# A hybrid decoder layer on one core: the second halo sum from raw weight rows, four steps moved in attention, and the y splits set ahead of the turns

## The chip, the cores and the metric

The kernel runs on one NeuronCore of a Trainium2 chip. The core has TensorE (matrix products, PE in the profile, with its weight loads as PEld), VectorE (DVE), ScalarE (ACT), GpSimd (POOL), and SyncE (SP), whose queue issues nearly all of this kernel's DMAs. The metric is the device time of one execution in microseconds (us), lower is better. The time shown is the median of three runs.

## The reference

One layer over 16 meta tokens and 1024 real tokens of width 1024, in float32. The parts around the change are these:

```python
h = jnp.concatenate([meta, x], axis=1)
for l in range(DEPTH):
    xn = rms_norm(h, mix_pre_g[l])
    proj = xn @ w_in[l]
    ...
    y_ssd = ssd_mixer(z, xbc, dt_raw, ssd_conv_w[l], ssd_conv_b[l], ssd_dt_bias[l],
                      ssd_a_log[l], ssd_d[l], ssd_norm_g[l])
    y_sb = rms_norm(stick_breaking_attention(q, k, v).reshape(Bsz, L, SB_WIDTH), sb_norm_g[l])
    mix = jnp.concatenate([y_ssd, y_sb], axis=-1) @ w_out[l]
    h = h + rms_norm(mix, mix_post_g[l])
    xn = rms_norm(h, ffn_pre_g[l])
    gu = xn @ w_up[l]
    g = causal_dwconv(gu[..., :D_FF], ffn_conv_w[l], ffn_conv_b[l])
    f = (jax.nn.gelu(g, approximate=True) * gu[..., D_FF:]) @ w_down[l]
    h = h + rms_norm(f, ffn_post_g[l])
return h[:, N_META:]
```

The product with `w_out` has 2048 rows: the first 1024 take the SSD output (half 0 in the kernel), the last 1024 the attention output (half 1). The convolution in the feed-forward part reaches two tokens back, so the last two meta tokens must also go through `w_out`, both norms and `w_up`. These two rows are the halo.

## The kernel before

Products that need precision split each float32 operand into a rounded part and a remainder and run three products (high by high, low by high, high by low). Such a split is a ScalarE copy (`yh`, `wh`) followed by a subtraction on GpSimd or VectorE (`yl`, `wl`).

**Attention (lines 989 to 1044).** Eight pairs of heads `p`, each with eight blocks `i` of 128 queries. For a block, `block_weights` computes scores on TensorE (z, two PSUM tiles shared with the transposes), two sigmoids on ScalarE, a scan on VectorE and a product on GpSimd. `block_turn` transposes the weights (tw, copied by ScalarE to th), and `block_mix` multiplies by the values (av). Between them, `fill` runs half chains of the next pair's projections (pj_q, pj_k, pj_v). `edge_turn` and `edge_mix` handle the columns that reach into the meta tokens: transposes twc, masks thc on VectorE, product avc. The order on TensorE is written out by hand here. The other engines are ordered by the planner of the tile framework, by program order among the instructions that it models as ready.

**First half of the output product.** From block (6, 2) on, `wout_steps` scales and splits rows of `w_out` half 0 (woa). From (7, 1) on, `ssd_half` (generator `first`) runs `out_steps` for eight tiles of 128 tokens: two halves of 512 columns, each 24 matmuls in two steps of 12, and after each half a copy `ma` on ScalarE and a store to `mixd`. It yields four times per tile; 22 of the 32 yields are used by the end of attention. `halo_rows` computes the two halo rows from the split weights: eight groups `k`, in each four products (high left, high right, low left, low right) with two output rows, in four column groups of the array; then two copies per column group to `mh` and a store of each to `halod`.

**Between the halves (lines 1068 to 1093).** Attention's pools close, and pools `op` (outp) and `est` open in the freed memory. The eight rows of `w_out` half 1 are loaded: two slots of the rotating buffer `wraw` and three of `est`. `second` scales and splits them (wohb, wolb), one row per step of `first`. `y0b` holds the attention output of the two halo tokens. After `first` ends, `halo_rows` runs for half 1, then `token_rstd` (ptb). On TensorE, too, the order is the planner's from the end of attention to tile 2.

**Second half of the output product (lines 1424 to 1496).** A loop over tiles t = 1 to 8. `out_steps` runs 2 x 24 matmuls; `ev2` on VectorE adds each half to `mt`, which holds half 0's product. `after` is the norm: square on ScalarE, root on GpSimd, scale (L1123) and add (L1124) on VectorE, a store, a second square, a second root, and `oxn` (L1133) on VectorE. `turn_x2` transposes `oxn` of an earlier tile (x2tp) and lets ScalarE and VectorE split it for the feed-forward part; for t = 0 it does so for the halo rows. `halo_sum` adds the four stored parts, `halo_norm` is `after` for the halo, and `edge_x2` prepares columns at the seams. `split_y` splits the attention output of the next tile. Its raw rows `yk` lie in `wraw`, which has two slots. From t = 2 on, the order on TensorE, VectorE, ScalarE and GpSimd is the program's; SP's order stays the planner's.

The feed-forward part follows. It is not changed.

Of the kernel before, what the change touches and what calls it, by code (L numbers as in the profile page):

```python
# [53 lines left out]
def tile_layer(ctx: ExitStack, tc: tile.TileContext, x, meta, rows, parts,  # L54
# [77 lines left out]
    yd1 = dr.tile([NT, P, 8, P], F32, name="yd1", tag="yd1")  # L132
    yh1 = dr.tile([P, 8, 2], F32, name="yh1", tag="yh1")
    mixd = [dr.tile([P, D], F32, name=f"mixd{t}", tag=f"mixd{t}") for t in range(NT)]
    halod = [dr.tile([2, D], F32, name=f"halod{n}", tag=f"halod{n}") for n in range(4)]
    zd = [dr.tile([4, P, L], F32, name=f"zd{g}", tag=f"zd{g}") for g in range(2)]
    xsd = [dr.tile([NT + 1, P, 512], F32, name=f"xsd{g}", tag=f"xsd{g}") for g in range(2)]
    mvd = dr.tile([NM, 8, P], F32, name="mvd", tag="mvd")
# [773 lines left out]
    def halo_rows(pool, half, y0, w, acc):  # L912
        for k in range(8):
            yield
            for c in range(4):
                mm(acc[32 * c:32 * c + 2, :], y0[:, k, :], w[k][c // 2][:, 512 * (c % 2):512 * (c % 2) + 512].bitcast(F32),
                   start=k == 0, stop=k == 7)
        for a in (0, 256):
            mh = pool.tile([P, 256], F32, tag="ma", name=f"mh{half}_{a}", bufs=1)
            for c in range(4):  # L920
                b = 512 * (c % 2) + a
                rows_ = slice(32 * c, 32 * c + 2)
                nc.scalar.activation(mh[rows_], acc[rows_, a:a + 256], AF.Copy)
                nc.sync.dma_start(out=halod[2 * half + c // 2][:, b:b + 256], in_=mh[rows_])
# [32 lines left out]
    def ssd_half(w, ys):  # L957
        for t in range(1, NT + 1):
            y = ys.pop(0)
            ma = stage_tile[0](f"ma{t}")  # L960

            def ev(acc, cs, t=t, ma=ma):
                nc.scalar.activation(ma[:, cs], acc, AF.Copy, scale=r_ssd[:, t:t + 1])  # L963
                nc.sync.dma_start(out=mixd[t - 1][:, cs], in_=ma[:, cs])

            for i, _ in enumerate(out_steps(0, t, w, y, ev)):
                if i == 1 and t < NT - 1:
                    ys.append(split_y(wp, 0, t + 2, ("whi", "wlo", WB)))
                yield

    wo1 = ExitStack()
    turn, mix = [], []
# [16 lines left out]
    for p in range(8):  # L989
        for i in range(NT):  # L990
            if p == 0 and i == 0:
                run(fill, 1)
            block = block_weights(p, i)
            next(block, None)
            if mix:
                block_mix(*mix.pop(0))
            if p > 0 and i == 3:
                edge_mix(p - 1, edge)
            run(fill, 1 + (i < FILL[p]))
            if first:  # L1000
                run(first, 1)
            run(block)
            if (p, i) == (7, 1):
                halo = halo_rows(ap, 0, y0a, wres, psum_mm("halo0"))
                run(halo, 3)
            ahead = iter(())
            if len(turn) > 2:
                ahead = begin_turn()
            if (p, i) == (7, 1):
                run(halo, 2)  # L1010
            if i < NT - 1:
                run(ahead)
            run(fill, int(p > 0 or i > 3))
            if (p, i) == (7, NT - 1):
                run(first, 1)
            run(ahead)
            if left[0] and wsteps is None:
                wres = []
                wsteps = wout_steps(third_slots(), 0, ssd_g, wres, [])
                y0a = halo_y(ap, 0)  # L1020
            if (p, i) == (6, 3):
                yk = [load_y(0, 1, rp.tile([P, L + 3], F32, tag="rq", name="yk0_1", bufs=3)[:, :D]
                             .rearrange("p (a b) -> p a b", b=P)),
                      load_y(0, 2, rp.tile([P, L], F32R, tag="rk", name="yk0_2", bufs=3).bitcast(F32)[:, :D]
                             .rearrange("p (a b) -> p a b", b=P))]
            if left[1] and not ys1:
                ys1.append(split_y(wp, 0, 1, ("whi", "wlo", WB), yk[0], nc.vector))
            for _ in range(2):
                if wsteps and len(wres) < min(8, 3 * left[0], STAGE.get((p, i), 0)):
                    run(wsteps, 1)  # L1030
            if wsteps and first is None and len(wres) == 8:
                run(wsteps)
                first = ssd_half(wres, ys1)
                run(first, 1)
                ys1.append(split_y(wp, 0, 2, ("whi", "wlo", WB), yk[1], nc.vector))
            elif first:
                run(first, 1)
                run(halo)
            if p == 7 and 2 < i < 6:
                run(meta_steps, 1)  # L1040
            if p == 0 and i == 2:
                token_rstd(r_ssd, ap, "a")
            if p > 0 and i == 2:
                edge = edge_turn(p - 1)
    while turn or mix:
        if mix:
            block_mix(*mix.pop(0))
# [25 lines left out]
    stage_tile[0] = lambda name: est.tile([P, D], F32, tag="mt", name=name)  # L1073
    wres2 = []
    y0b = halo_y(op, 1)
    ahead = [raw_w(1, k, None if k % 5 < 2 else est.tile([P, D], F32, tag="wr", name=f"worb{k}", bufs=3)) for k in range(8)]
    second = wout_steps(own_slots(op), 1, sb_g, wres2, ahead)
    run(second, 1)
    ys = [split_y(op, 1, 1, ("yh", "yl", 2))]
    for _ in first:  # L1080
        run(second, 1)
    run(second)
    ys.append(split_y(op, 1, 2, ("yh", "yl", 2)))

# [2 lines left out]
    for t in (1, 2):  # L1087
        mts.append(wp_f32("whi" if t == 1 else "wlo", f"mb{t}"))
        nc.sync.dma_start(out=mts[-1], in_=mixd[t - 1])
    run(halo_rows(est, 1, y0b, wres2, psum_fa("halo1")[:, 0, :]))  # L1090
    wo1.close()
    xpool.close()
    token_rstd(r_sb, op, "b")
# [98 lines left out]
    nc.sync.dma_start(out=halo_xt, in_=meta[M0:NM, :])  # L1192

    def halo_sum(n):
        r = (r_ssd, r_ssd, r_sb, r_sb)[n][:2, 0:1]
        if n == 0:
            nc.vector.tensor_scalar(halo_mt, halo_mt, r, None, op0=ALU.mult)
        else:
            nc.vector.scalar_tensor_tensor(halo_mt, halo_mo, r, halo_mt, op0=ALU.mult, op1=ALU.add)
        if n < 3:  # L1200
            nc.sync.dma_start(out=halo_mo, in_=halod[n + 1])

    nc.sync.dma_start(out=halo_mt, in_=halod[0])
# [220 lines left out]
    for t in range(1, NT + 1):  # L1424
        if t == 2:
            order.enter_context(tc.manual_schedule(engines=ORDERED))
        if 1 < t < NT - 1:
            yk = load_y(1, t + 1, yraw[0](f"yk1_{t + 1}"))
        if mts:
            mt = mts.pop(0)  # L1430
        else:
# [16 lines left out]
        steps = out_steps(1, t, wres2, ys.pop(0), ev2)  # L1448
        run(steps, 2)
        run(norm, 1)  # L1450
        if len(pend) > 1:
            turn = pend.pop(0)()
            run(turn, 2)
# [2 lines left out]
                run(steps)  # L1456
            run(turn)
        run(norm)
        if 1 < t < NT - 1:
            ys.append(split_y(op, 1, t + 1, ("yh", "yl", 2), yk, nc.vector if t < 5 else nc.gpsimd))  # L1460
        if t == 2:
            halo_sum(2)
        elif t == 3:
            halo_sum(3)
            halo_norm = after(0, halo_mt, 2, halo_xt, halo_mo, halo_mo)
            run(halo_norm, 1)
        elif t == 4:
            run(halo_norm)
# [11 lines left out]
        if t == NT:  # L1480
            break
        if t == 6:
            ys.append(split_y(op, 1, NT, ("yh", "yl", 2)))
        xn = f1.tile([P, 1032], F32, tag="fa", name=f"oxn{t}")[:, :D]
        junk = psum_fa(f"jk{t}").rearrange("p a b -> p (a b)")
        norm = after(t, mt, P, xt, xn, junk)
# [4 lines left out]
        pend.append(lambda t=t, xn=xn: turn_x2(t, P, xn, x2_tiles(t)))  # L1491
        if t == 3:
            run(halo_norm, 2)
        elif t == 4:
            run(turn_x2(0, 2, halo_mo, x2_tiles(0)))
    opool.close()
    tA, tB = ExitStack(), ExitStack()
# [372 lines left out]
```

## Time and profile before

| what | value |
|---|---|
| median of three runs | 1745.74 us (1743.22 to 1745.97) |
| the profiled execution | 1741.94 us |
| its span, first to last instruction | 1740.0 us |
| mean granted TensorE clock | 0.997 |
| TensorE busy in the span | 1707.8 us |
| VectorE, ScalarE, GpSimd busy | 1121.2, 822.9, 857.9 us |
| attention pairs 6 and 7 with the first half of the output product | about 770 to 959 us |
| halo sum of half 1 on TensorE | 959.5 to 966.3 us |
| second half of the output product | 968.2 to 1075 us |

In a timeline row, the columns are the start, the duration, the engine, the line, the operation, and the tiles written and read, with the idle time just before and what ended it in brackets. A row with xN merges N neighbours. In a row of waits the columns are the total, how often, and the longest. The window table has busy time per engine (with counts), the granted clock, the share of the DMA engines, and GB/s.

### The profile page before, as it was taken

The page shows a single profiled execution, that of the slowest core. Times are in us where ns is not written, and L with a number is a line of the kernel's source. Part 1 is how long each engine was busy: PE and PEld are TensorE (multiplying, and loading weights), DVE is VectorE, ACT ScalarE, POOL GpSimd, SP SyncE. Part 2 cuts the span into 40 slices and gives each one's busy share as a digit, 9 for nine tenths or more (in the row PEclk, how much of TensorE's full clock was granted, in tenths as well). Part 3 has the DMA queues.
Part 4 walks back from the last instruction along what each step waited for, and adds up shares of the span by engine and source line. Part 5 has one row for each costly group of instructions (what it writes and reads, how often), then busy time and mean ns, then how long its engine had stood idle before and what let it go on. Part 6 is the DMA issues. An engine that isn't in the chain of part 4 may idle for free.

```text
span 1740.0 us, 28052 instructions
## 1 busy us (share of the span) xinstructions
PE 1707.8 (98%) x11230; PEld 1496.6 (86%) x11230; DVE 1121.2 (64%) x1230; ACT 822.9 (47%) x1374; POOL 857.9 (49%) x645
## 2 busy tenths in 40 slices
PE   7999999999999999999999979999999999999998
PEld 6999889888999998998687768999988888887886
DVE  5752964775676677668532457676666666658777
ACT  5423653545566566558553234533333333343544
POOL 4323663686565566555552124487776777400001
PEclk9999999999999999999999999999999999999999
DMA  4233343231011011122215443232332222395335
GB/s 163 63 110 98 98 135 109 65 95 38 26 37 45 30 37 32 31 62 73 82 57 199 165 145 122 67 116 97 105 108 91 92 91 91 108 322 199 104 110 181
DMA packets 90694, 173.88 MB, mean 100 GB/s; under 512 B 10714, under 2 KB 35834, under 8 KB 90564
## 3 DMA queue, kind: packets, MB, share of 16 engines
q1 hardware_dynamic: 90564, 172.10, 31.2%
q8 instruction: 88, 1.44, 0.4%
q14 instruction: 42, 0.34, 0.1%
HBM read 122.33 MB, written 49.73 MB: 99 GB/s over the span
## 4 chain that ended last, share of the span: by engine, by line
PE 89%; issue 3%; DVE 3%; ACT 2%; POOL 2%; DMA 1%; POOLq 0%; DVEq 0%; SPq 0%; ACTq 0%
PE fX L1280 10%; PE dnA L1690 7%; PE fY L1280 6%; PE fA L1280 6%; PE mo L951 6%; PE pj_k L165 5%; PE pj_v L165 5%; PE pj_z L165 5%; PE dnB L1690 5%; PE pj_q L165 5%; PE pj_X L165 5%; PE av L802 4%; PE z L765 3%; PE tw L787 3%; PE pj_B L165 1%
## 5 line engine op out<-in xcount | busy, mean ns | idle before, releaser
L775 POOL TENSOR_TENSOR bt<-bt,kp 128x256 f32<-128x256 f32 (+7 forms) x128 | 213.0, 1683 | 185.5 <-DVE kp L773 135.2
L773 DVE TENSOR_TENSOR_SCAN kp<-kp,hold 128x272 f32<-128x272 f32 (+7 forms) x128 | 183.4, 1473 | 25.3 <-ACT kp L766 15.0
L1223 POOL TENSOR_TENSOR wlo<-wr,whi 128x1024 fp32r<-128x1024 f32 x43 | 107.9, 2518 | 38.4 <-ACT whi L1222 38.4
L1727 POOL TENSOR_TENSOR fms<-fms 128x1 f32<-128x1 f32 x8 | 3.2, 394 | 223.4 <-ACT dh L1612 197.0
L766 ACT ACTIVATE kp<-z 128x288 f32<-128x288 f32 (+6 forms) x112 | 82.6, 737 | 50.9 <-PE z L765 27.5
L1222 ACT ACTIVATE whi<-wr 128x1024 fp32r<-128x1024 f32 x43 | 45.6, 1060 | 111.6 <-PE fX L1280 68.3
L165 PE MATMUL pj_v<-xs,wh_v 128*128 128x400 f32 (+2 forms) x384 | 94.9, 334 | 0.0
L1352 DVE SCALAR_TENSOR_TENSOR ga<-gr,pp,ga 128x1024 f32<-128x1024 f32 x44 | 72.3, 1643 | 34.9 <-ACT ga L1345 34.1
L165 PE MATMUL pj_k<-xs,wh_k 128*128 128x400 f32 (+2 forms) x384 | 94.5, 333 | 0.0
L165 PE MATMUL pj_q<-xs,wh_q 128*128 128x386 f32 (+2 forms) x384 | 93.9, 331 | 0.0
L789 ACT ACTIVATE th<-tw 128x1024 f32<-128x1024 f32 (+2 forms) x96 | 75.6, 816 | 38.5 <-PE tw L787 38.4
L1612 ACT ACTIVATE dh<-ar 128x512 fp32r<-128x512 f32 x77 | 48.5, 630 | 92.7 <-PE dnB L1690 44.7
L165 PE MATMUL pj_X<-xs,wh_X 128*128 128x400 f32 (+2 forms) x384 | 92.0, 327 | 0.2 <-ACT craw_X L211 0.2
L165 PE MATMUL pj_z<-xs,wh_z 128*128 128x386 f32 (+2 forms) x384 | 91.5, 326 | 0.0
L951 PE MATMUL mo<-woa,yh 128*128 128x512 f32 x256 | 84.4, 398 | 2.1 <-ACT ma L963 1.2
L1613 DVE TENSOR_TENSOR dl<-ar,dh 128x512 fp32r<-128x512 f32 x77 | 53.2, 692 | 50.4 <-ACT dh L1612 50.3
L741 DVE CAST qh<-q 128x128 fp32r<-128x128 f32 x64 | 45.7, 715 | 59.7 <-PE z L765 59.4
L767 ACT ACTIVATE bt<-z 128x288 f32<-128x288 f32 (+6 forms) x112 | 82.9, 740 | 0.0
L802 PE MATMUL av<-th,v 128*64 128x128 f32 x1152 | 77.2, 278 | 0.0
L787 PE MATMUL tw<-ident,bt 128*128 128x128 f32 x576 | 75.7, 274 | 0.9 <-ACT bt L767 0.5
L802 PEld LDWEIGHTS av<-th,v 128*64 128x64 f32 x1152 | 61.5, 136 | 13.8 <-issue 11.1
L787 PEld LDWEIGHTS tw<-ident,bt 128*128 128x128 f32 x576 | 65.5, 141 | 7.1 <-issue 3.3
(558 smaller groups left out, 5648.8 us busy)
## 6 DMA issues: line engine op xcount, KB each, us to landing
wr<-in_w_up SPq DMA_DIRECT2D x44, 512.0 KB
fds<-ga SPq DMA_DIRECT2D x44, 256.0 KB
b<-in_w_down SPq DMA_DIRECT2D x44, 256.0 KB
ar<-fds SPq DMA_DIRECT2D x44, 256.0 KB
fda<-ga SPq DMA_DIRECT2D x33, 256.0 KB
ar<-fda SPq DMA_DIRECT2D x33, 256.0 KB
yk<-yd SPq DMA_DIRECT2D x16, 512.0 KB
wor<-in_w_out SPq DMA_DIRECT2D x12, 512.0 KB
```

The costliest lines, as they stand in the source:

```text
L165: mm(acc[:ncol, :n - s], a[:, k, :ncol], xs[c0][:, b, k, s:n], start=(k == 0 and j == 0), stop=(k == KB - 1 and j == 2))
L766: nc.scalar.activation(kp[:, :, a:a + w], z[:, :, :w], AF.Sigmoid, scale=-QSCALE)
L767: nc.scalar.activation(bt[:, :, a:a + w], z[:, :, :w], AF.Sigmoid, scale=QSCALE)
L773: nc.vector.tensor_tensor_scan(kp[:, j][:, ::-1], kp[:, j][:, ::-1], hold[:, L - n:L][:, ::-1], 0.0, op0=ALU.mult, op1=ALU.max)
L775: nc.gpsimd.tensor_tensor(bt[:, j, 0:m], bt[:, j, 0:m], kp[:, j, 1:m + 1], op=ALU.mult)
L787: nc.tensor.transpose(tw[:, j, b, :], bt[:, j, c0:c0 + P], ident)
L789: nc.scalar.activation(th[:, :, :nb, :], tw[:, :, :nb, :], AF.Copy)
L802: mm(av[halves[j], :], v[:, kb, halves[j]], th[:, j, b, :], start=kb == 0, stop=kb == i)
L951: mm(acc, u[:, k, :], v[:, cs], start=(k == 0 and j == 0), stop=(k == 7 and j == 2))
L1223: nc.gpsimd.tensor_tensor(l, raw, h.bitcast(F32), op=ALU.subtract)
L1280: mm(acc[:, c, :nn], u[:, k, :], v[:, k, c0:c0 + nn], start=first and k == 0 and j == 0, stop=k == 3 and j == 2, skip_group_check=not first)
L1690: mm(banks[BANK[n], t], u[:, 0, c], v[:, 1, :], start=(n in (1, 2, 5) and p == 0 and i == 0), stop=(p == NPR - 1 and i == 2), skip_group_c ...
```

## The change

The second halo sum no longer waits for the split rows. It multiplies the raw rows `worb` by `y0g`, which is `y0b` times the gain `sb_g`. Each group has four products of 256 columns and adds into one PSUM tile; the groups are given during `first`, whenever rows have been handed to the split. There is then one copy per column group, and `halod` and `halo_sum` have three parts instead of four.

`first` now yields 0 before and 1 behind a chain's copy, and two weight rows are given behind each such copy instead of one at every step. `est` has four slots for rows.

In attention, the fill at (6, 6) comes ahead of the transposes, `edge_turn` comes ahead of the weight rows and of `first`, the rest of the first halo sum comes ahead of `first`, and `mh` has two buffers.

In the loop, `yk` of tile 3 is loaded at t = 1, ahead of `x`. Each later split stands right behind the second root, ahead of the turn, followed by the load for the tile after. The halo's turn moves from t = 4 to t = 5.

```diff
-    halod = [dr.tile([2, D], F32, name=f"halod{n}", tag=f"halod{n}") for n in range(4)]
+    halod = [dr.tile([2, D], F32, name=f"halod{n}", tag=f"halod{n}") for n in range(3)]
...
-            mh = pool.tile([P, 256], F32, tag="ma", name=f"mh{half}_{a}", bufs=1)
+            mh = pool.tile([P, 256], F32, tag="ma", name=f"mh{half}_{a}", bufs=2)
...
-                yield
+                yield i % 2
...
             ahead = iter(())
+            if (p, i) == (6, 6):
+                run(fill, 1)
             if len(turn) > 2:
                 ahead = begin_turn()
...
-            run(fill, int(p > 0 or i > 3))
+            run(fill, int((p > 0 or i > 3) and (p, i) != (6, 6)))
...
+            if p > 0 and i == 2:
+                edge = edge_turn(p - 1)
             for _ in range(2):
                 if wsteps and len(wres) < min(8, 3 * left[0], STAGE.get((p, i), 0)):
                     run(wsteps, 1)
...
             elif first:
+                run(halo)
                 run(first, 1)
-                run(halo)
...
-            if p > 0 and i == 2:
-                edge = edge_turn(p - 1)
...
-    ahead = [raw_w(1, k, None if k % 5 < 2 else est.tile([P, D], F32, tag="wr", name=f"worb{k}", bufs=3)) for k in range(8)]
+    ahead = [raw_w(1, k, None if k % 6 < 2 else est.tile([P, D], F32, tag="wr", name=f"worb{k}", bufs=4)) for k in range(8)]
+    worb = list(ahead)
     second = wout_steps(own_slots(op), 1, sb_g, wres2, ahead)
     run(second, 1)
     ys = [split_y(op, 1, 1, ("yh", "yl", 2))]
-    for _ in first:
-        run(second, 1)
+    y0g = op.tile([P, 8, 2], F32, tag="y0g", name="y0g", bufs=1)
+    nc.vector.tensor_tensor(y0g, y0b, sb_g.unsqueeze(2).to_broadcast([P, 8, 2]), op=ALU.mult)
+    acc = psum_fa("halo1")[:, 0, 0:256]
+    summed = []
+
+    def halo_raw():
+        k = len(summed)
+        summed.append(k)
+        for c in range(4):
+            mm(acc[32 * c:32 * c + 2, :], y0g[:, k, :], worb[k][:, 256 * c:256 * c + 256], start=k == 0, stop=k == 7)
+
+    for i in first:
+        rows_in = len(wres2)
+        if i == 1:
+            run(second, 2)
+        while len(summed) < rows_in:
+            halo_raw()
     run(second)
...
-    run(halo_rows(est, 1, y0b, wres2, psum_fa("halo1")[:, 0, :]))
+    while len(summed) < 8:
+        halo_raw()
+    mh = est.tile([P, 256], F32, tag="ma", name="mh1", bufs=1)
+    for c in range(4):
+        rows_ = slice(32 * c, 32 * c + 2)
+        nc.scalar.activation(mh[rows_], acc[rows_, :], AF.Copy)
+        nc.sync.dma_start(out=halod[2][:, 256 * c:256 * c + 256], in_=mh[rows_])
...
-        r = (r_ssd, r_ssd, r_sb, r_sb)[n][:2, 0:1]
+        r = (r_ssd, r_ssd, r_sb)[n][:2, 0:1]
...
-        if n < 3:
+        if n < 2:
             nc.sync.dma_start(out=halo_mo, in_=halod[n + 1])
...
-        if 1 < t < NT - 1:
-            yk = load_y(1, t + 1, yraw[0](f"yk1_{t + 1}"))
+        if t == 1:
+            yk = load_y(1, 3, yraw[0]("yk1_3"))
...
         run(steps, 2)
         run(norm, 1)
+        if 1 < t < NT - 1:
+            ys.append(split_y(op, 1, t + 1, ("yh", "yl", 2), yk, nc.vector if t < 5 else nc.gpsimd))
+            yk = load_y(1, t + 2, yraw[0](f"yk1_{t + 2}"))
         if len(pend) > 1:
...
         run(norm)
-        if 1 < t < NT - 1:
-            ys.append(split_y(op, 1, t + 1, ("yh", "yl", 2), yk, nc.vector if t < 5 else nc.gpsimd))
         if t == 2:
             halo_sum(2)
         elif t == 3:
-            halo_sum(3)
             halo_norm = after(0, halo_mt, 2, halo_xt, halo_mo, halo_mo)
...
         if t == 6:
-            ys.append(split_y(op, 1, NT, ("yh", "yl", 2)))
+            ys.append(split_y(op, 1, NT, ("yh", "yl", 2), yk))
...
-        elif t == 4:
+        elif t == 5:
             run(turn_x2(0, 2, halo_mo, x2_tiles(0)))
```

## Prediction

> **What bounds the kernel now.** I read the page's head, then who waited for whom on TensorE, then a table of windows and the chain of work around the longest wait, then each engine's timeline there.
>
> ```profile
> span 1740.0 us, 28052 instructions
> PE 1707.8 (98%) x11230; PEld 1496.6 (86%) x11230; DVE 1121.2 (64%) x1230; ACT 822.9 (47%) x1374; POOL 857.9 (49%) x645
> ```
> ```profile
> PE x2tp L1139 <- DVE mo L1133: 5.9, 1, 5.9
> PE mo L951 <- POOL yl L939: 2.9, 2, 1.5
> PE mo L951 <- DVE yl L939: 1.5, 1, 1.5
> PE mo L951 <- ACT ma L963: 1.2, 2, 0.7
> PE avc L822 <- DVE qh L741: 1.2, 1, 1.2
> PE mo L951 <- ACT mh L923: 0.9, 1, 0.9
> PE tw L787 <- ACT bt L767: 0.5, 1, 0.5
> PE tw L787 <- issue: 0.4, 1, 0.4
> ```
> TensorE is the bound: at 98% busy, the time changes by TensorE work removed and by TensorE waits opened or closed, and little else. These eight rows are 14.5 us together and lie between 785 and 1052 us, where the diff works. The longest, the turn of the two halo rows, also leaves a slow clock behind it:
>
> ```profile
> 1015.46:1021.56 6.10, 0.16 (x1) 0.81 0.19 66
> 1021.56:1026.30 4.74, 4.74 (x17) 0.52 0.71 246
> ```
> ```profile
> 1022.54 7.37 PE mo L951 x24
> ...
> 1069.71 5.47 PE mo L951 x24
> ```
> The granted clock behind the gap was 0.52, and the same 24 matmuls took 7.37 us instead of 5.47. The halo turn therefore cost 5.9 + 1.9 = 7.8 us.
>
> **Edge turn and the order at pair 6.** VectorE's order in attention is the planner's, by program order among what is ready:
>
> ```profile
> 783.88 1.28 DVE L888 SCALAR_TENSOR_TENSOR woa<-wor,pp,woa 128x1024 fp32r<-128x1024 f32 x1 [1.40 <-ACT woa L887]
> 785.08 0.75 DVE L814 TENSOR_TENSOR thc<-twc,cmask 128x256 f32<-128x256 f32 x2
> ```
> A weight split of 1.28 us stood ahead of the edge masks, and TensorE waited 1.2 us for them. Written first, the masks go first: gain 1.2 us (bounds 0 and 1.2). The split they push back by 0.75 us is on no wait's account: no row names woa as the releaser of mo. At block (6, 6) a half chain of projection moves from behind the transposes to ahead of them. It covers the two waits (0.9 us), but it no longer stands between the transposes and the next block:
>
> ```profile
> 810.32 0.44 PE L787 MATMUL tw<-ident,bt 128*128 128x128 f32 x2 [0.53 <-ACT bt L767]
> 812.12 0.43 PE L765 MATMUL z<-kh,qh 64*128 64x348 f32 x2
> ```
> ```profile
> 810.26 1.36 ACT L789 ACTIVATE th<-tw 128x1024 f32<-128x1024 f32 x2
> ```
> That block's scores need a PSUM bank which ScalarE's copy of the transposes frees. The transposes would end near 810.9, the larger copy (about 1.0 of the 1.36) near 811.8, so z starts at 811.8 instead of 812.12: gain 0.3 us (bounds 0 and 0.9).
>
> **First halo sum.** The rest of halo0 goes ahead of the second half of tile 1, and its two copies get a buffer each. The halo bank and the tile's bank then no longer meet: of the ma waits the one near 842 (1.2 - 0.7 = 0.5) and the mh wait (0.9) go, 1.4 us (bounds 0 and 1.4). Nothing is queued behind the earlier copies but sigmoids that wait for TensorE anyway.
>
> **Second halo sum.** Before, 64 matmul records of 512 columns ran alone between the two output products:
>
> ```profile
> 959.45 0.60 PE L916 MATMUL halo<-wohb,y 128*2 128x512 f32 x2
> ...
> 959.88 0.60 PE L916 MATMUL halo<-wohb,y 128*2 128x512 f32 x2
> ...
> 966.32 2.07 PE L445 MATMUL ptb<-ones,sq 128*2 128x1 f32 x18
> ```
> Four records, one per column group, every 0.43 us, 6.87 us in all. After, the raw rows are summed (the gain moves into y0, one VectorE product of 128x16): 64 records of 256 columns, half the columns, 3.43 us less if columns set the pace and 0 if a fixed cost per record does. I take the half, since the pace is 0.21 us per 512 columns and group. The sum is now given in about five visits. One visit shows its price in the first halo sum:
>
> ```profile
> 844.86 3.62 PE L916 MATMUL halo<-woa,y 128*2 128x512 f32 x32
> 848.41 0.44 PE L811 MATMUL twc<-ident,cb 128*128 128x128 f32 x2
> ```
> 3.55 us for 32 records that need 8 x 0.43 = 3.44, and some 0.1 at the entry: 0.2 a visit, four visits more, 0.8 us. Gain 3.4 - 0.8 = 2.6 us. The copies fall from eight to four, as do their DMAs on SP; both ran beside tile 1, so nothing.
>
> ScalarE gives weight rows behind a chain's copy now, so the second ma wait (0.7) should go: 0.6 (bounds 0 and 0.7).
>
> Against this, TensorE's queue gets a new wait. Up to 979 its order is the planner's, and a halo group behind a late load holds all output products behind it.
>
> ```profile
> 937.50 6.67 DMA mixd<-ma
> ```
> ```profile
> 944.34 1.15 ACT L887 ACTIVATE wohb<-wor,pp 128x1024 fp32r<-128x1024 f32 x1 [1.37 <-DMA mixd<-ma]
> ...
> 951.97 1.15 ACT L887 ACTIVATE wohb<-wor,pp 128x1024 fp32r<-128x1024 f32 x1 [1.37 <-DMA wor<-in_w_out]
> ```
> ```profile
> 944.19 0.32 SPq L909 DMA_DIRECT2D y<-yh  x1
> ...
> 946.83 0.33 SPq L875 DMA_DIRECT2D wor<-in_w_out  x1
> ...
> 969.78 1.43 SPq L924 DMA_DIRECT2D halod<-mh  x4
> ...
> 973.62 0.22 SPq L1201 DMA_DIRECT2D mo<-halod  x1
> ```
> The pool that holds y0 and the scaled rows opens when the mixd store lands, at 944.2. y0 is issued then; the small halod store landed some 2.4 us after its issue (971.2 to 973.6), so y0g stands near 947 and no group can run before it. Rows 6 and 7 reuse the buffers of rows 0 and 1, so they load only when groups 0 and 1 have read them, and one such load took 946.8 to 952.0, 5.1 us. The planner misjudged this load before: ScalarE idled 1.37 us for it with a ready copy behind. I charge 1.5 us, about one such error; bounds 0 (all hidden) and 12 (rival 3). Row 5 loads early in the fourth buffer; its 512 KB may hold back the store in flight, at most by a load's 5.1 us, and the last split would still meet TensorE no earlier than the 22nd matmul of tile 1.
>
> **The loop over tiles 2 to 8** has a fixed order on four engines. The halo turn moves from tile 4 to tile 5, one halo accumulation goes, and each y split stands ahead of the turn's copies. Gone: 7.8 for the halo turn, and 1.5 for yl of tile 4, whose split gets ahead of a normalisation (1.28 us, the oxn row below) and the two subtractions with their waits: 9.3 us. What is late next is VectorE:
>
> ```profile
> 1003.62 1.27 DVE L1199 SCALAR_TENSOR_TENSOR mb<-mo,r_sb,mb 2x1024 f32<-2x1024 f32 x1
> ...
> 1013.06 0.73 DVE L1436 SCALAR_TENSOR_TENSOR mb<-mo,r_sb,mb 128x512 f32<-128x512 f32 x1
> ...
> 1021.34 0.73 DVE L1436 SCALAR_TENSOR_TENSOR mb<-mo,r_sb,mb 128x512 f32<-128x512 f32 x1
> ```
> ```profile
> 1027.94 0.19 ACT L1129 ACTIVATION_READ_ACCUMULATOR jk<-mb 128x1 f32 x1
> ...
> 1033.65 1.06 ACT L938 ACTIVATE yh<-yk 128x1024 fp32r<-128x1024 f32 x1
> ```
> ```profile
> 858.71 2.37 POOL L939 TENSOR_TENSOR yl<-yk,yh 128x1024 fp32r<-128x1024 f32 x1
> ...
> 1034.79 3.12 POOL L939 TENSOR_TENSOR yl<-yk,yh 128x1024 fp32r<-128x1024 f32 x1 [5.70 <-ACT yh L938]
> ```
> In the clock of before: without the 1.27 and with the tile's square no longer behind the halo's, 1013.06 becomes 1011. yl5 then ends near 1014.6, asked at 1014.2: 0.6 us with the wake-up. The second accumulation of tile 4 still stands behind all of tile 2's turn and the halo's last step, 1019.3 instead of 1021.3, while TensorE is over 9 us ahead of its old place. From that accumulation to the square's end took 1021.34 to 1028.13; yh now follows at once (1.06) and then yl on GpSimd (3.12), 11.05 us with the gaps: yl6 at 1030.3. TensorE, through tile 5 (twice 5.47 and a turn of 0.87, from 1014.7) and the halo turn (about as long), asks at 1027.4. A wait of 2.9 takes the place of 1.5: +1.4. The same count one tile on gives yl7 a wait of 1.2 for 1.5: -0.3. Last, the turn of tile 8:
>
> ```profile
> 1085.59 1.28 DVE L1133 SCALAR_TENSOR_TENSOR oxn<-mb,rs_ff,gffn 128x1024 f32<-128x1024 f32 x1 [0.45 <-POOL rs_ff L192]
> ```
> ```profile
> 1087.58 0.87 PE x2tp L1139 x8
> ```
> It had 0.7 us to spare (1086.87 to 1087.58). The other engines gain some 2 us less than TensorE by then: +1.5 (bounds 0 and 2.5). Net 9.3 - 0.6 - 1.4 + 0.3 - 1.5 = 6.1 us (bounds 3 and 9).
>
> A wait of 2.9 us lies between gaps seen: 1.5 left the clock whole, 5.9 halved it, so 0 to 1.9 us more. I take 0. [...]
>
> **Sum.** 1.2 + 0.3 + 1.4 + 0.6 + 2.6 - 1.5 + 6.1 = 10.7 us. The profiled execution took 1741.94 us (span 1740.0 and 1.94 around it), so 1731.2; the median shown, 1745.74, is 3.8 above it, so about 1735.
>
> **Rivals.**
> 1. Everything hides: the planner places the halo groups behind ready data and yl6 comes in time. The sum gains the 1.5, 1.4 and 1.5 back: 15 us, 1730.6. For it: GpSimd took 3.12 us in that split but 2.37 in another. Against: VectorE's order still puts tile 4's accumulation last.
> 2. The chain through VectorE and GpSimd becomes the pace: yl6 waits 4 us and the clock falls (+1.1 + 1.9), the last turn waits 2.5 (+1): 6.7 us gained, 1739. For it: the other engines' chain shortens by only 2 us.
> 3. Slower: the second halo sum blocks TensorE. If group 0 is queued where it is written, behind tile 6's last product at 936.8, TensorE waits until 947: 10.1 us and 1.9 of slow clock; rows 6 and 7 then load behind it and each can hold the queue, at most 5.1 us apiece. From 12.2 us of such waits on (10.7 + 1.5) it beats all gains, beyond 15.7 it shows; at 17, 1750. For it: the planner's error at 951.97. Against: wohb at 944.34 waits for the same store and was late by only those 1.37 us.
> 4. The waits only change place (halo groups 6 to 8 us late, or attention gains nothing): 1743, no change.
>
> **How the numbers follow.** Forecast 0.50, rival 1 0.18, rival 2 0.12, rival 3 0.12, rival 4 0.08. 0.2% is 3.5 us, so faster means under 1742.2: 0.50 + 0.18 + 0.12 = 0.80; same 0.08; slower 0.12. The range runs from 1727 (loop at its bound of 9 with rival 1) to 1744 (rival 4 in, rival 3 out). The forecast's own is 1731 to 1739.
>
> **What would show it.** No TensorE wait of 5.9 us at the halo turn and clock 1.0 through the loop; yl6 the longest remaining wait, near 3 us; halo records of 256 columns in some five groups, 3.4 us together; no mh or avc wait. A TensorE wait above 5 us between 930 and 965, or yl waits beyond 5 us together, would make it wrong.

## The result, and the profile after

| | before | after |
|---|---|---|
| median | 1745.51 us (1743.22 to 1745.97, 4 executions) | 1736.46 us (1735.12 to 1739.4, 4 executions) |
| ratio of the times | | 0.995, 95% interval 0.9935 to 0.9966 |
| profiled execution, span | 1741.94, 1740.0 us | 1735.83, 1733.7 us |
| clock over the span | 0.997 | 0.995 |

The kernel became faster by 9.0 us in the medians. The two profiled executions differ by only 6.1, and a good part of this section is about those other 3 us.

The head of the page and TensorE's list of waits (us in total, times, the longest), of the changed kernel:

```profile
span 1733.7 us, 28039 instructions
PE 1708.7 (99%) x11230; PEld 1498.9 (86%) x11230; DVE 1114.4 (64%) x1230; ACT 821.6 (47%) x1370; POOL 858.3 (50%) x645
```
```profile
PE mo L951 <- POOL yl L939: 1.9, 1, 1.9
PE z L765 <- ACT th L789: 1.9, 1, 1.9
PE halo L1092 <- POOL yl L939: 1.3, 1, 1.3
PE avc L822 <- DVE qh L741: 1.0, 1, 1.0
...
PE mo L951 <- DVE tmsb L449: 0.4, 1, 0.4
PE x2tp L1163 <- DVE oxn L1157: 0.3, 1, 0.3
```

The eight waits of before were 14.5 us; these six are 6.8. The 5.9 us at the halo turn, the ma and mh waits and two of the three yl waits are gone. Four waits are new: z at block (6, 6), the first halo group, the first product of tile 1 behind ptb (`tmsb` is VectorE's copy of ptb), and the last turn.

The busy time of TensorE did not fall with them, although the second halo sum takes 3.0 us less. One reason is the clock. The columns of the next view are the stretch and its length, then for PE, PEld, DVE, ACT and POOL the busy time and count, then the granted clock, the DMA share and GB/s. The changed kernel:

```profile
873.60:877.00 3.40, 3.40 (x27) 2.92 (x27) 0.34 (x2) 0.19 (x1) 3.40 (x4) 1.00 0.00 0
877.00:880.40 3.40, 3.40 (x25) 2.44 (x23) 0.32 (x1) 3.03 (x5) 1.57 (x5) 0.50 0.42 135
...
965.70:969.10 3.40, 2.99 (x20) 2.70 (x21) 0.22 (x2) 0.28 (x1) 1.51 (x1) 1.00 0.50 149
969.10:972.50 3.40, 3.40 (x9) 2.61 (x8) 0.00 (x0) 0.00 (x0) 0.32 (x1) 0.51 0.96 331
1027.20:1030.60 3.40, 1.83 (x13) 1.09 (x11) 0.69 (x1) 2.64 (x6) 2.85 (x3) 1.00 0.90 292
1030.60:1034.00 3.40, 3.06 (x7) 2.48 (x8) 2.54 (x3) 0.74 (x3) 0.29 (x1) 0.50 0.48 154
1034.00:1037.40 3.40, 3.40 (x16) 2.72 (x16) 1.29 (x1) 1.08 (x2) 0.79 (x2) 1.00 0.86 306
```

The reader is to see stretches of half clock, each about 3.41 us long, so that each costs about 1.7 us if TensorE is busy throughout (in the one at 969, output products begin every 0.43 us, behind it every 0.23). This execution has four of them up to the last tail (from 54.37, 876.98, 969.14 and 1030.58), before had one of double length, behind the halo turn. Only the one at 1030 stands behind a loop wait. The one at 969 stands behind ptb's 18 one-column products and the 0.4 us wait after them. Those at 54 and 877 stand in code that the change does not touch. So the two profiles alone understate the change, and the runs below are compared by stage with the half clock taken out.

A second reason is the pace of the output products. The next view has the 96 products of tile 1's second half to tile 3's first half, which run without a wait: before, the changed kernel, and y0_early, a run described below that differs from the changed kernel only in the pool of two small tiles. The window's length is what to read; its count has one product of the chain before.

```profile
973.80:995.56 21.76, 21.76 (x97) 17.83 (x95) 4.17 (x5) 0.00 (x0) 1.00 0.33 105
```
```profile
974.84:997.06 22.22, 22.22 (x97) 17.88 (x95) 5.54 (x6) 0.00 (x0) 1.00 0.32 108
```
```profile
976.57:998.33 21.76, 21.76 (x97) 17.84 (x95) 5.54 (x6) 0.00 (x0) 1.00 0.34 112
```

The same 96 products take 21.76 us in before, loop_only, rows_old and y0_early, and 22.22 in the ten other kernels of the table below, at full clock in all. The ten are those that hold the new tile `y0g` in the pool `op`; the four have no such tile, or have it in the pool `wp`. TensorE's working time in stage B (see below), at full clock, is 1.2 us longer in the ten on average. In y0_early the slower pace is found in the first half of the output product instead: 22.97 us for four chains of 24 products, 22.54 in every other kernel. So it cost about 1.2 us in which pool tiles of 64 bytes a partition lie. How they slow the products is not shown.

**How the stages are measured.** Stage A runs from the edge product of pair 6 (first avc) to the first product of tile 1 in the second half. Stage B runs from there to the last turn (x2tp). Both ends are starts of rows in TensorE's timeline. "Half clock" is the time at granted clock 0.5 inside the stage. Half of it, as far as TensorE was at work in it, is subtracted to give the length at full clock: in before, 2.3 of the 6.8 us behind the halo turn fell into its wait and cost nothing.

| kernel | median us | ratio to before (95% interval) | A raw, half clock, full | B raw, half clock, full |
|---|---|---|---|---|
| before | 1745.5 | | 182.3, 0, **182.3** | 119.2, 6.8, **116.9** |
| after | 1736.5 | 0.9950 (0.9935 to 0.9966) | 181.3, 3.4, **179.6** | 113.5, 6.8, **110.2** |
| loop_only | 1737.1 | 0.9961 (0.9948 to 0.9975) | 184.8, 3.4, **183.1** | 112.7, 3.4, **111.0** |
| no_loop | 1742.7 | 0.9990 (0.9982 to 0.9999) | 182.6, 6.8, **179.2** | 118.7, 6.8, **116.1** |
| fill_old | 1733.8 | 0.9944 (0.9931 to 0.9956) | 180.6, 3.4, **178.9** | 111.9, 3.4, **110.2** |
| rows_old | 1737.0 | 0.9963 (0.9950 to 0.9976) | 183.3, 3.4, **181.6** | 112.7, 3.4, **111.0** |
| y6_early | 1737.9 | 0.9956 (0.9938 to 0.9973) | 183.5, 6.8, **180.0** | 114.4, 3.4, **112.7** |
| y0_early | 1737.6 | 0.9958 (0.9946 to 0.9970) | 181.9, 3.4, **180.2** | 113.0, 6.8, **109.8** |
| turn_t4 | 1740.2 | 0.9972 (0.9962 to 0.9981) | 186.4, 10.2, **181.6** | 115.2, 6.8, **112.5** |
| split_late | 1738.9 | 0.9961 (0.9949 to 0.9973) | 179.9, 0, **179.9** | 117.1, 6.8, **114.0** |
| y6_dve | 1732.4 | 0.9938 (0.9925 to 0.9950) | 184.2, 6.8, **181.1** | 111.4, 3.4, **109.7** |
| y1_dve | 1736.5 | 0.9951 (0.9938 to 0.9964) | 182.9, 6.8, **179.5** | 113.4, 3.4, **111.7** |
| best | 1729.0 | 0.9909 (0.9895 to 0.9923) | 179.1, 0, **179.1** | 111.3, 3.4, **109.6** |
| best2 | 1726.6 | 0.9886 (0.9870 to 0.9903) | 177.2, 0, **177.2** | 109.7, 0, **109.7** |

Six kernels share A's code: after, no_loop, y6_early, split_late, turn_t4 and y6_dve. The first four lie within 179.2 to 180.0. The other two have a wait of TensorE's transposes for GpSimd (1.4 and 0.9 us) that the four don't have, as loop_only has one of 1.2. So A and B, from one profile of each kernel, resolve about one us where such a wait is told apart.

The medians resolve less. Each run was timed beside executions of the kernel before, whose median went from 1744.2 to 1746.2 us. So where two runs are compared below, the difference of their ratios is given behind the difference of their medians. Each ratio is known to 1.5 to 3 us, so a difference below some 3 us is not resolved. At full clock, the change takes 2.7 us from A and 6.7 from B, 9.4 together.

### The profile page after: what moved, and what is told of

Same layout as the page of the kernel before. It is cut to its first block, busy times and chain, and to the rows that moved or that the text cites. A ratio compares the mean times of both kernels' runs of the same rounds, so it can differ in the third digit from the quotient of the medians.

```text
span 1733.7 us, 28039 instructions
## 1 busy us (share of the span) xinstructions
PE 1708.7 (99%) x11230; PEld 1498.9 (86%) x11230; DVE 1114.4 (64%) x1230; ACT 821.6 (47%) x1370; POOL 858.3 (50%) x645
```

## The experiments

**loop_only and no_loop.** The two halves of the change, each by itself. loop_only is the kernel before with the diff's last five places alone (load of y one tile ahead, splits ahead of the turns, halo turn at tile 5); no_loop is the changed kernel with these five undone.

> The kernel before with nothing but the loop over tiles 2 to 8 changed (y splits ahead of the turns, the halo turn at tile 5); the second halo sum is the old one, so its accumulation of 1.27 us on VectorE stays. Theory of the prediction: the loop is worth 6.1 us, about 1 of it comes from the accumulation that is gone, so about 5 us faster than the kernel before, near 1740.5. Rival, from the trace of the changed kernel: the edits ahead of the loop pay each other back and the loop carries everything, so about 9 us faster, near 1736.5. In both the wait of 5.9 us at the halo turn is gone; under the prediction VectorE is late next and a yl wait of 3 us or more stands at tile 5 or 6.

> The changed kernel with the loop as before (halo turn at tile 4, y splits behind the turns), all edits ahead of it kept. Theory of the prediction: 10.7 - 6.1 = 4.6 us faster than the kernel before, near 1741, and the 5.9 us wait shrinks by the 1.27 us accumulation. Rival: nothing is left but that accumulation, 0 to 2 us, 1744 to 1745.5.

Measured: the loop alone 6.8 us faster than before by its ratio, everything else alone 1.7. Together 8.5, against the 8.7 of the whole change by its ratio: the halves add up. By stage, the loop takes B from 116.9 to 111.0, and the other edits take A from 182.3 to 179.2. The first run lies halfway between its two expectations (5 and 9 us), the second within its rival's 0 to 2. Yet the edits ahead of the loop do not pay each other back: 3.1 us in A and 0.8 in B. Of these 3.9 the medians show 1.5. Part of the rest can be clock (mean 0.9947 over no_loop's executions, 0.9955 over those of before beside them, by the slope at the end of the document 1.0 us); the remaining 1.4 us are within the interval of the ratio. The halo turn's wait fell to 4.3 us in no_loop, by 1.6, where the accumulation that is gone was expected to take 1.27.

**turn_t4 and split_late.** The loop's two moves, each undone alone.

```diff
-        elif t == 5:
+        elif t == 4:
             run(turn_x2(0, 2, halo_mo, x2_tiles(0)))
```
```diff
         run(norm, 1)
-        if 1 < t < NT - 1:
-            ys.append(split_y(...))
-            yk = load_y(1, t + 2, ...)
         if len(pend) > 1:
...
         run(norm)
+        if 1 < t < NT - 1:
+            ys.append(split_y(...))
+            yk = load_y(1, t + 2, ...)
```

> The changed kernel with the halo turn back at tile 4, y splits still ahead of the turns. Theory (place of the turn is the main term): a wait of 5 to 5.9 us at the halo turn with half clock behind it returns and the 1.9 us wait at tile 6 with its half clock goes: 4 to 5 us slower than the changed kernel. Rival (the accumulation that is gone and the earlier splits are the main term): the halo turn's wait is 1 to 2 us and the kernel at most 1.5 us slower.

> The changed kernel with the y splits back behind the turns (block loads still one tile ahead, halo turn at tile 5). Theory: three yl waits of about 1.5 us return in place of one of 1.9 with half clock behind it: 2.6 us slower if clock isn't counted, about 1 us slower if it is (waits of 1.5 left the clock whole). Rival: VectorE's and ScalarE's earlier copies of the turns pull in later work, no difference beyond 0.5 us.

Measured: turn_t4 3.7 us slower than the changed kernel in the medians (3.8 by the ratios), split_late 2.4 (1.9, not resolved). TensorE's waits in turn_t4, and in split_late:

```profile
PE x2tp L1163 <- DVE mo L1157: 5.3, 1, 5.3
```
```profile
PE mo L951 <- DVE yl L939: 2.9, 2, 1.6
PE mo L951 <- POOL yl L939: 1.9, 2, 1.3
...
PE mo L951 <- ACT yh L938: 0.9, 1, 0.9
```

Moved back, the turn waits its 5.3 us again, although one accumulation is gone and the splits are early: its place is what counts. But no yl wait is left there, so B at full clock rises only by 2.3 (110.2 to 112.5). Behind this wait the half clock lasts 6.8 us, behind the yl wait of the changed kernel 3.4; how much of the loss that makes is not told apart. With the splits back behind the turns, waits of 5.7 us return in place of 2.3 (the yl wait and the last turn), and B rises by 3.8. The prediction had put 7.8 us on the turn and 1.5 on the splits. By stage the splits are worth more than the turn, by the medians less, and by neither so little.

**rows_old.** The second halo sum as in the kernel before, with its eight copies and its second accumulation.

> The changed kernel with the second halo sum as before (split rows, 64 records of 512 columns in one stretch, eight copies, two accumulations, three early row buffers), all else changed. Theory of the prediction: the raw rows gain 2.6 - 1.5 = 1.1 us and the ma wait 0.6 stays gained or not with the old order of rows, and one accumulation on VectorE is worth about 1 in the loop: 1 to 2.7 us slower than the changed kernel. Rival: the new waits ahead of tile 1 (1.3 for the group, the pool 2 us later) eat all of it: no difference beyond 0.5 us.

Measured: A is 181.6 instead of 179.6, B 111.0 instead of 110.2; a wait of 1.4 us of mo for ma is back. The raw rows are worth 2.0 us in A. In B they are worth 0.7 net: the waits there sum to 4.2 us here and 2.3 in the changed kernel, so the accumulation that they save is worth some 1.9, and the slower pace that came with `y0g` takes 1.2 of it back. The run is 0.6 us slower in the medians (2.3 by the ratios), which does not resolve this.

**fill_old.** The projection at (6, 6) back behind the transposes.

> The changed kernel with the projection at block (6, 6) back behind the transposes. Theory of the prediction (the edit gains 0.3 us): 0.3 us slower than the changed kernel. Rival, from its trace (a wait of 1.86 us at the scores in place of two of 0.9 together): about 0.6 to 1.0 us faster than the changed kernel, and the wait of z for th is gone while tw waits 0.5 and 0.4 again.

Measured: 2.6 us faster than the changed kernel in the medians (1.0 by the ratios, not resolved), 0.7 by A. The wait of z is gone and tw's two are back (0.5 each), as the rival has it. The clock was higher too: 0.998 over the executions of fill_old, 0.996 over those of the changed kernel. ScalarE's timeline in the changed kernel shows why z waits there:

```profile
810.81 1.09 ACT L938 ACTIVATE yh<-yk 128x1024 fp32r<-128x1024 f32 x1
811.76 0.42 ACT L388 ACTIVATE kh<-pj_k 128x256 fp32r<-128x256 f32 x1
812.03 1.34 ACT L789 ACTIVATE th<-tw 128x1024 f32<-128x1024 f32 x2
```

The two copies of the transposes stand behind a y split and the copy of the projection that now comes first. They start at 812.0 instead of 810.3, and z waits 1.86 us for their bank.

**y0_early and y1_dve.** Two ways to remove the wait of the first halo group: y0 and its product in a pool that is open long before, or one engine exchanged.

```diff
-    y0b = halo_y(op, 1)
+    y0b = halo_y(wp, 1)
...
-    y0g = op.tile([P, 8, 2], F32, tag="y0g", name="y0g", bufs=1)
+    y0g = wp.tile([P, 8, 2], F32, tag="y0g", name="y0g", bufs=1)
```
```diff
-    ys = [split_y(op, 1, 1, ("yh", "yl", 2))]
+    ys = [split_y(op, 1, 1, ("yh", "yl", 2), eng=nc.vector)]
```

> The changed kernel with the two halo rows of y (y0) and their product with the gain (y0g) in a pool that is open long before, so that they no longer wait for the pool which opens behind the store of mixed rows at 946. Theory: the wait of 0.9 to 1.3 us at the first halo group is this and goes, the groups stand one by one behind the raw rows: 1 to 1.5 us faster than the changed kernel. Rival: the groups then wait for late raw rows instead, in TensorE's planned order: no gain, or up to 2 us slower.

> The changed kernel with one engine exchanged: tile 1's y split subtracts on VectorE instead of GpSimd. Theory (the product of 128x16 for y0g took 2.02 us because GpSimd's subtraction held it up until its own end): the product takes under 0.3 us and the wait of the first halo group falls from 1.3 us to under 0.6; 0.7 to 1.3 us faster than the changed kernel. Rival: the product's 2 us are its own (a small product with a broadcast operand is slow) and stay; no gain.

VectorE's row for the product, first in the changed kernel with GpSimd's row beside it, then in y1_dve:

```profile
949.10 2.02 DVE L1084 TENSOR_TENSOR y0g<-y,pp 128x16 f32<-128x16 f32 x1 [0.25 <-DMA y<-yh]
```
```profile
948.61 2.48 POOL L939 TENSOR_TENSOR yl<-yk,yh 128x1024 fp32r<-128x1024 f32 x1 [12.81 <-ACT yh L938]
```
```profile
954.13 0.17 DVE L1084 TENSOR_TENSOR y0g<-y,pp 128x16 f32<-128x16 f32 x1
```

The product of 128x16 took 2.02 us, until GpSimd's subtraction ended (951.09), and 0.17 without it. The first group's wait falls from 1.26 to nothing, as the theory said. Yet neither run is faster. In y1_dve, the stretch from the last edge turn (twc) to tile 1 is 1.1 us shorter, and then B is 1.4 longer: yl waits of 2.8 in place of 1.9, and 0.7 in place of 0.3 at the last turn. The loop takes the us back; the likely reason, not tested, is that VectorE, ScalarE and GpSimd come no sooner. In y0_early the wait is gone as well, but A is 0.6 longer. The groups stand in six visits instead of four, 4.12 us in place of 3.89. More than that, the two tiles in `wp` brought the slower pace to the first output product, 0.43 us for each 96 of its 384 products; in B it is gone, and more waiting (1.1 us) takes most of that back.

**y6_early and y6_dve.** The longest wait left, yl of tile 6. Both place its split, and that of tile 7, at the end of tile 4 (5): y6_early ahead of the tile's second square, on GpSimd as before, y6_dve ahead of the first square, on VectorE. The diff is that of y6_dve.

```diff
-        if 1 < t < NT - 1:
+        if 1 < t < 5:
             ys.append(split_y(...))
             yk = load_y(1, t + 2, ...)
...
+        if t in (4, 5):
+            ys.append(split_y(op, 1, t + 2, ("yh", "yl", 2), yk, nc.vector))
+            yk = load_y(1, t + 3, yraw[0](f"yk1_{t + 3}"))
         xn = f1.tile([P, 1032], F32, tag="fa", name=f"oxn{t}")[:, :D]
```

> The changed kernel with the split of tile 6's y block (and of tile 7's) given one place earlier: at the end of tile 4 (5), ahead of that tile's second square on ScalarE. Theory, clock counted: the wait of 1.9 us at tile 6 goes, and so does the 3.41 us of half clock seen behind it in three profiles of three (1.7 us): 3 to 3.6 us faster than the changed kernel. Rival 1, the prediction's reading that a wait under 2.9 us costs no clock: 1.9 us faster. Rival 2: the wait only moves to yl of tile 7 or to the last turn, whose normalisation is then late: under 1 us faster.

> The changed kernel with the splits of tiles 6 and 7's y blocks ahead of the first square of tiles 4 and 5, and their subtraction on VectorE instead of GpSimd. Theory (VectorE's normalisations of 1.28 us took 3.5 in the last such try because GpSimd's subtraction of 2.4 us ran beside them, and both engines have idle room before the first square): no yl wait at tile 6, normalisations at 1.3 us, no 3.41 us of half clock near 1030; the wait of 1.9 and its 1.7 of clock gone, 3 to 3.6 us faster than the changed kernel. Rival 1: VectorE is the pace of the loop, 1.2 us more on it a tile appears at the turns: under 1 us faster. Rival 2: the long normalisations have another cause and stay at 3.5 us.

y6_early gained nothing: its median is 1.4 us above the changed kernel's (1.0 by the ratios) and its B 2.4 longer. The split came early enough, but VectorE's and GpSimd's timelines there show what it cost:

```profile
1023.79 3.52 DVE L1147 SCALAR_TENSOR_TENSOR mb<-mb,rs_mo,gpost 128x1024 f32<-128x1024 f32 x1 [2.23 <-POOL rs_mo L192]
1027.35 1.23 DVE L1148 TENSOR_TENSOR mb<-mb,xr 128x1024 f32<-128x1024 f32 x1
```
```profile
1023.83 2.41 POOL L939 TENSOR_TENSOR yl<-yk,yh 128x1024 fp32r<-128x1024 f32 x1
```

A normalisation that takes 1.28 us in y6_dve took 3.52: it began beside GpSimd's subtraction, and ended 1.1 us behind that one's end. The square behind it came late, and the halo turn waited 1.8 us and tile 7 2.5. In y6_dve the same normalisation takes 1.28 and no yl wait is left. It is 4.1 us faster than the changed kernel in the medians, but 2.1 by the ratios, whose intervals overlap. At full clock, B falls by only 0.5, since the last turn now waits 1.5 us for VectorE (rival 1). The half clock near 1030 is gone with the wait; what of the rest is that and what is chance is open.

**best.** fill_old and y6_dve together with two more edits: the edge turn's transposes ahead of a projection, and the narrow products of the meta rows (avm) in two halves in two blocks.

```diff
+            if p > 0 and i == 2:
+                edge = edge_turn(p - 1)
             run(fill, int(p > 0 or i > 3))
...
-        for p in range(8):
-            mm(av[:, 4 * p:4 * p + 4], mv[:, p, :], ...)
+        for h4 in (0, 4):
+            av = psum_tp("avm1")[:, 0, :] if h4 else psum_av("avm")
+            for p in range(h4, h4 + 4):
+                mm(av[:, 4 * p:4 * p + 4], mv[:, p, :], ...)
...
+            if h4 == 0:
+                yield
```

> Four edits of the changed kernel together, each readable at its own place: the projection at (6, 6) back behind the transposes, the transposes of the edge turn ahead of a projection, tile 6's and 7's splits early and on VectorE, and the 16 narrow matmuls of the meta rows (avm, 1.87 us in one stretch) in two halves of 8 in two blocks. Theory: z's wait of 1.9 gone for 0.9 at tw, no avc wait (1.0), no yl wait with half clock (3.3), and no half clock near 877, which followed the whole stretch in 8 of 10 profiles (1.4 on average): about 6.5 us faster than the changed kernel, near 1730. Rival: the half clock near 877 has no link to the narrow stretch and comes all the same; the edge order pays back elsewhere: 2 to 4 us faster.

Measured 1729.0 us, 7.4 below the changed kernel (7.2 by the ratios), with no avc wait, no z wait, and no half clock between 860 and 960. VectorE's order at pair 6 is what the diff's edge move was to give:

```profile
781.74 1.82 DVE L892 SCALAR_TENSOR_TENSOR woa<-wor,pp,woa 128x1024 fp32r<-128x1024 f32 x1
783.49 0.74 DVE L814 TENSOR_TENSOR thc<-twc,cmask 128x256 f32<-128x256 f32 x2
784.81 1.28 DVE L892 SCALAR_TENSOR_TENSOR woa<-wor,pp,woa 128x1024 fp32r<-128x1024 f32 x1 [0.58 <-ACT woa L891]
```

**best2.** best with y1_dve's exchange, and with the 18 one-column products of ptb in two stretches of 10 and 8 with output products between.

> The four edits of the run called best and two more: tile 1's y split subtracts on VectorE (the product of 128x16 then took 0.17 us instead of 2.02 in its own run), and the 18 one-column matmuls of the second half's norm (ptb, 1.93 us in one stretch, 0.4 of wait behind it) in two stretches of 10 and 8 with output products between. Theory: the first halo group's wait of 0.9 us goes, the wait of 0.4 behind ptb goes or halves, and no half clock follows ptb, which it did in 5 of 13 profiles (0.65 us on average): 1.5 to 2 us faster than best, 1727 to 1728, with no half clock between 940 and 1080. Rival: one-us waits and the order of raw rows trade places as in the runs with earlier y0 rows: within 0.7 us of best, and a half clock near 970 again.

Measured 1726.6 us, 2.5 below best (4.0 by the ratios) and 9.9 below the changed kernel (11.2), and no half clock from 20 us to the tail. Its four executions lie within 0.9 us of each other. The windows of its profile:

```profile
860.00:925.00 65.00, 65.00 (x442) 53.13 (x442) 18.03 (x17) 29.35 (x43) 28.21 (x20) 1.00 0.19 66
925.00:968.00 43.00, 43.00 (x245) 32.43 (x244) 13.12 (x14) 17.02 (x21) 8.17 (x4) 1.00 0.69 230
968.00:1090.00 122.00, 120.27 (x649) 102.16 (x648) 84.08 (x92) 54.85 (x88) 29.32 (x41) 1.00 0.42 141
```

TensorE is busy for the whole of the first two stretches, and the 1.7 us missing in the third are the last turn's 1.5 and one of 0.2. The next gain in this region would have to come from there, on VectorE, or from the pace: best2 is among the ten with the slower products. No run here closes either.

## Why the prediction was right, point by point

The forecast was 1735 and the measured median 1736.5. The sum of 10.7 us came out as 9.0. That it came so close is in part luck: the terms deviate more than the sum does, the loop upwards, the clock, the edge masks, the fill and a pace that no term had downwards.

- **TensorE is the bound.** Right: 99% busy after.
- **The loop, 6.1 us.** Its mechanism was right, its size too small. Raw B without the half clock behind ptb at 969 went from 119.2 to 111.8, 7.4 us; loop_only, which keeps the second accumulation, gives 7. Of the waits named as late next, yl6 was 1.9 instead of 2.9 (GpSimd took 2.35 us, not 3.12), yl5 and yl7 did not come, and the last turn's was 0.3 instead of 1.5. The division between turn (7.8) and splits (1.5) was wrong. Undone alone, the turn costs 3.7 us in the medians and 2.3 in B, the splits 2.4 and 3.8. Both sums are 6.1, near the 6.2 and 5.8 of both undone together (no_loop), so the parts add up, only not to the shares that were forecast.
- **"I take 0" for the clock behind that wait.** The 0 was the author's choice between the two gaps seen, and this step failed: a wait of 1.9 us was followed by 3.41 us at half clock in this profile and in fill_old, rows_old and y0_early. Of five profiles with this wait only y1_dve's stayed whole. The sign "clock 1.0 through the loop" did not come, and rival 2's half clock behind yl6 came at less than half its wait.
- **Second halo sum, 2.6 for the records, -1.5 for new waits, 0.6 for ma.** 1.7 predicted, 2.0 measured by rows_old. The records take 3.89 us in four visits in place of 6.87, where 3.4 and 0.8 were forecast. The new wait was 1.26, near the 1.5 that was charged, but its cause was another: not a late raw row, but y0g, whose product took 2.02 us beside GpSimd's subtraction and 0.17 in y1_dve. The store to mixd came later with the fourth early row, as the prediction had allowed. SyncE's queue in the changed kernel:

```profile
935.83 1.76 SPq L875 DMA_DIRECT2D worb<-in_w_out  x4
...
938.22 5.72 SPq L964 DMA_DIRECT2D mixd<-ma  x2
...
946.28 0.32 SPq L909 DMA_DIRECT2D y<-yh  x1
```

The pool opens, and y0 is issued, 8.06 us behind the issue of the store; before it was 6.69 (937.50 to 944.19), and in rows_old, with three early rows again, 6.39 (938.73 to 945.12).
- **A term that the sum lacks.** The new tile `y0g` was counted as one VectorE product. The loop's output products became slower with it (22.22 us for 96 of them in place of 21.76), about 1.2 us over the loop.
- **First halo sum, 1.4.** Its waits are gone from the list. A's 2.7 us, less the 2.0 of the second sum, plus the 0.7 that the fill lost, leave 1.4; no run undoes this edit alone.
- **Edge masks, 1.2.** Failed. The premise was that program order decides among what is ready; VectorE's planned order still had the weight split ahead of the masks, and the wait went from 1.2 to 1.0. In the changed kernel:

```profile
784.27 1.28 DVE L888 SCALAR_TENSOR_TENSOR woa<-wor,pp,woa 128x1024 fp32r<-128x1024 f32 x1 [1.28 <-ACT woa L887]
785.48 0.75 DVE L814 TENSOR_TENSOR thc<-twc,cmask 128x256 f32<-128x256 f32 x2
```
It took transposes that are ready earlier (best) to put the masks first.
- **Fill at (6, 6), 0.3.** Failed, with the other sign: -0.7. The step that broke was "the larger copy near 811.8", which left out what the same edit puts ahead of that copy on ScalarE.

Neither the slower rival nor rivals 1 and 2 came: no halo group waited for a late row, and VectorE became a bound only in the versions that went further.

## What to carry to other kernels

When two engines feed a third, moving one wait shows the next one behind it: undo each part of a change alone and count the stages, since the total can be right while its parts are not. A new tile, however small, is part of the change: compare the pace of code that nobody touched. Before giving work to GpSimd to relieve VectorE, look at what VectorE runs at that moment, since it can lose more than it gave away: a normalisation took 3.52 us instead of 1.28 beside a subtraction of tile 6's y block in y6_early, and that subtraction takes VectorE 1.2 us in y6_dve. And where a few us matter, take the clock out of the comparison first: a stage at full clock resolved about one us here, when medians over five executions did not.

## What the runs showed of the hardware

**The half clock came on a raster.** Within one execution, the stretches of half clock start at multiples of one distance: in the changed kernel 54.37, 876.98, 969.14 and 1030.58 are 241, 27 and 18 steps of 3.413 us apart, and in y1_dve 418.1, 817.5, 882.3 and 971.1 are 117, 19 and 26. The raster lies differently from execution to execution: counted from the first instruction, its first step begins at 3.2 us in the profile of the changed kernel, at 2.1 in that of before, at 1.7 in y1_dve and at 0.3 in y6_dve. So the same code can meet it well or badly. A narrow stretch in untouched code (avm, 16 products of 4 columns, 1.87 us) was followed by half clock in 9 of the 12 profiles that have it whole, and in neither of the two that have it in parts; the 18 one-column products of ptb in 5 of the 10 profiles that have them whole with a wait of 0.4 us behind them, and in none of the 3 without the wait. Waits were followed by it too. Of the steps at full clock between 790 and 1046 us in all profiles, those with 1.5 us or more of waiting in them were followed by half clock in 14 of 17 cases, those with 1.3 to 1.5 us in 1 of 7, and those with less only behind avm and ptb.

**Most of the scatter goes with it.** Over 49 executions of the kernel before, the mean time falls with the clock over the span: 1746.2 us at 0.993 (one execution), 1746.4 at 0.994 (14), 1745.3 at 0.995 (11), 1743.7 at 0.996 (20), 1742.1 at 0.997 (3). A straight line through them falls by 1.3 us for 0.001 of clock and takes up 0.64 of the variance. best2, without half clock from 20 us on in its profile, scatters by 0.9 us.

**Side by side, VectorE or GpSimd took longer.** Rows above: VectorE took 2.02 us against 0.17 and 3.52 against 1.28, and ended 0.03 and 1.1 us behind GpSimd's end. The other way round, the prediction's GpSimd row of 3.12 us began at 1034.79, while VectorE normalised until 1035.68 (in 1.28 us), and the same subtraction took 2.35 in the changed kernel (from 1028.54), with no normalisation beside it. What holds the one up is not shown.
